# Second token group of a two-layer hybrid decoder: the trunk after the linear attention on two-part weights and data, and a layer norm written in place

## The chip, the cores and the metric

One core of one Trainium2 chip runs the whole step. The metric is the device time of one execution in microseconds (us). Five engines work side by side, each through its own queue in order: TensorE (PE in the rows, its weight loads PEld), VectorE (DVE), ScalarE (ACT), GpSimd (POOL) and SyncE (SP), which issues most transfers.

## The reference, cut to what matters

Two layers run over 512 prompt tokens and 64 sample tokens of width 1024. Each layer is a trunk and a channel mixer:

```
proj = x @ w_in + b_in                      # split among the mixers and the gates
A: windowed attention   B: GLA linear attention   C: causal pooling
oB = rmsnorm(gla) * silu(gb)
merged = sum_i sigmoid(gate_i) * (branch_i @ w_branch_i)
x = LN(alpha * x + merged @ w_out)
x = LN(alpha * x + peer(x))                 # product-key experts, top 16 of 16384
```

All of it is float32 in the reference.

## The kernel before

The tokens are cut into two groups. Group 0 is 256 prompt tokens and the 64 sample tokens (W = 320), group 1 the other 256 prompt tokens (W = 256, `G.fin`). In each layer `_p1` runs the trunk for group 0, the query of the channel mixer is computed for it, then `_p1` runs for group 1 and its query follows; then comes a long stretch over 128 blocks of experts.

A trunk weight is a tile of 128 x 1024 (512 KB, eight blocks of 128 x 128), fetched by `w_get` from the table `wall`, through a ring of three buffers per name. There are two ways to multiply with it (`passes`, L174; `mm_into`, L178):

- Group 0 uses two-part operands. `stream` (L132) loads `raw`, ScalarE casts it to `whi` (fp32r, L130), and VectorE forms `wlo = raw - whi` (L127). Data are split likewise into a high and a low part. Each of the eight blocks takes three matmuls: high by high, high by low, low by high. That is 24 matmuls per tile.
- Group 1 uses plain float32 (`G.nat`): `raw` goes to TensorE as it lands, with one float32 matmul per block. The trace shows each of these as two records.

The query tiles (`pq`) are split for both groups, on GpSimd in group 1.

The order of group 1's trunk: attention with its gate `ga` and its branch product `wa`; `_phase_gla` (qb, kb, vb and the chunked scan); `_phase_gla_out` (eight `gb` tiles, L573); `_branch` with eight `gbr` and eight `wb` tiles (L230); `_phase_pool` (eight `uc` tiles, L629, and two `wp` tiles used in parts, L615); `_branch` with eight `gc` and eight `wc` tiles; `_phase_out` (eight `wo` tiles, L742, then `_ln` and the transposes at L708). From `gb` on this is 58 tiles a layer.

While group 1's trunk runs, group 0's selection and spread run in the background: each `w_get` calls `tick`, which issues about one background step (`set_bg`, L1122, about 100 steps for about 100 tiles). A spread step is one comparison over 128 x 512 on VectorE (`jo`, L930), four of 128 x 128 (`io`, L936), four float32 matmuls (L940), and four ScalarE copies into `gst` (L942); every eighth step writes four `gst` tiles to memory (`gd`, L948), and each of these tiles has one buffer. Some steps also gather a row of experts (`uvr`) and weigh it on VectorE (L994, L1001). Background work stands behind the trunk in the planner's priorities, weight loads and splits stand ahead of it (`PRIO`, 95). The framework's planner sets the final order of every engine's queue before the run by its own estimates.

Of the kernel before, what the change touches and what calls it, by code (L numbers as in the profile page):

```python
# [10 lines left out]
F32 = mybir.dt.float32  # L11
F32R = mybir.dt.float32r
# [59 lines left out]
WPOS = {n: i for i, n in enumerate(PLAN)}  # L72
# [34 lines left out]
class Net:  # L107
# [59 lines left out]
    def w_get(self, l, name, pool=None):  # L167
        self.tick()
        with self.tc.high_priority(PRIO):
            return self.stream(self.I["wall"][l, WPOS[name]], self.nc.vector if self.G.smp else self.nc.gpsimd, pool,  # L170
                               whole=self.G.nat and name[0] != "pq")

    @staticmethod
    def passes(w):  # L174
# [45 lines left out]
def _gate(n, l, gname, m, th):  # L220
    psg = n.mm(n.w_get(l, (gname, m)), n.xs, n.G.W)
    b = BPOS[gname, m]
    n.nc.scalar.activation(th, psg, AF.Tanh, scale=0.5, bias=n.hb[:, b:b + 1])


def _branch(n, l, gname, wname, o, first):
    nc, W = n.nc, n.G.W
    with n.tc.tile_pool(name="br_" + gname, bufs=3, side="right" if gname == "gbr" else "left") as up:
        n.up = up
        for m in range(8):  # L230
            dst = n.merged[m // 4][:, m % 4, :]
            if not first:
                th = n.unit("th")
                _gate(n, l, gname, m, th)
            psb = n.mm(n.w_get(l, (wname, m)), o, W)
            if first:
                nc.vector.scalar_tensor_tensor(dst, dst, 1.0, psb, op0=OP.add, op1=OP.mult)
            else:
                nc.vector.scalar_tensor_tensor(th, th, 1.0, psb, op0=OP.add, op1=OP.mult)
                nc.gpsimd.tensor_tensor(dst, dst, th, op=OP.add)  # L240
# [440 lines left out]
def _ln(n, p, z, m, gb, out):  # L681
    nc = n.nc
    st = p.tile([128, 2, nc.vector.BN_STATS_DIM], F32, name="bst", bufs=2)
    for i in range(2):
        nc.vector.bn_stats(st[0:m, i, :], z[0:m, i * 512:(i + 1) * 512])
    mv = p.tile([128, 4], F32, name="mv", bufs=2)
    nc.vector.bn_aggr(mv[0:m, 0:2], st[0:m])
    nc.vector.tensor_scalar(mv[0:m, 2:3], mv[0:m, 1:2], LN_EPS, None, op0=OP.add)
    nc.scalar.activation(mv[0:m, 2:3], mv[0:m, 2:3], AF.Sqrt)
    nc.vector.scalar_tensor_tensor(z[0:m], z[0:m], mv[0:m, 0:1], gb[0:m, 0, :], op0=OP.subtract, op1=OP.mult)  # L690
    nc.vector.reciprocal(mv[0:m, 3:4], mv[0:m, 2:3])
    nc.vector.scalar_tensor_tensor(out[0:m], z[0:m], mv[0:m, 3:4], gb[0:m, 1, :], op0=OP.mult, op1=OP.add)
# [10 lines left out]
def _transpose_tok(n, x, m, new_ps, dsts):  # L703
    nc, c = n.nc, n.c
    for q in range(2):
        pt = new_ps()
        for k in range(4):
            nc.tensor.transpose(pt[:, k, 0:m], x[0:m, (4 * q + k) * 128:(4 * q + k + 1) * 128], c["ident"][0:m, 0:m])  # L708
        for xh, xl, c0 in dsts:
            if xl is None:  # L710
                nc.scalar.copy(xh[q][:, :, c0:c0 + m], pt[:, :, 0:m])
            else:
                n.split(xh[q][:, :, c0:c0 + m], xl[q][:, :, c0:c0 + m], pt[:, :, 0:m])


def _phase_out(n, l, xres, dsts):
    tc, nc, G = n.tc, n.nc, n.G
    mp = n.parts("m")
    for m in range(8):
        q, k = m // 4, m % 4  # L720
        nc.scalar.activation(mp[0][q][:, k, :], n.merged[q][:, k, :], AF.Copy, scale=0.5)
        if len(mp) > 1:
            nc.vector.scalar_tensor_tensor(mp[1][q][:, k, :], n.merged[q][:, k, :], 0.5, mp[0][q][:, k, :].bitcast(F32),
                                           op0=OP.mult, op1=OP.subtract)
    ms = [n.ks(t) for t in mp]
    if n.G.smp:
        nc.scalar.dma_start(n.O["s_pool"][l, :, 7:15, :], n.us.rearrange("(b s) c -> b s c", b=NB))
    with tc.tile_pool(name="out", bufs=1) as p:
        gb = _ln_rows(n, p, l, 1)
        zs = []  # L730
        for t, c0, m in G.tok:
            z = p.tile([128, 1024], F32, name=f"z{t}")
            nc.sync.dma_start(z[0:m], xres[t * 128:t * 128 + m, :])
            zs.append(z)
        def block(q, blk, tok):
            (t, c0, m), z = tok
            ps = n.pmm.tile([128, 512], F32, tag="mm", name="ps_wo", bufs=3)
            pa = n.passes(blk[0])
            for a, (wi, xi) in enumerate(pa):
                for k in range(8):  # L740
                    w = blk[k // 4][wi].rearrange("p (k c) -> p k c", k=4)[:, k % 4, :]
                    nc.tensor.matmul(ps[0:m, 0:256], ms[xi][k][:, c0:c0 + m], w,  # L742
                                     start=(a == 0 and k == 0), stop=(a == len(pa) - 1 and k == 7))
            zc = z[0:m, q * 256:(q + 1) * 256]
            nc.vector.scalar_tensor_tensor(zc, zc, ALPHA, ps[0:m, 0:256], op0=OP.mult, op1=OP.add)

        toks = list(zip(G.tok, zs))
        with ExitStack() as wctx:
            late = wctx.enter_context(tc.tile_pool(name="wlate", bufs=4)) if G.smp else None
            for qs in ((0,), (1,), (2, 3)) if G.smp else ((0,), (1,), (2,), (3,)):  # L750
                blks = [[n.w_get(l, ("wo", 2 * q + i), late if len(qs) > 1 else None) for i in range(2)] for q in qs]
                for tok in toks:
                    for q, blk in zip(qs, blks):
                        block(q, blk, tok)
        for (t, c0, m), z in zip(G.tok, zs):
            x = p.tile([128, 1024], F32, name="x1", bufs=2)
            _ln(n, p, z, m, gb, x)
            nc.scalar.dma_start(n.x1d[t * 128:t * 128 + m, :], x[0:m])
            _transpose_tok(n, x, m, lambda: n.sm("pt"), dsts(t, c0))


def _p1(n, l, G, xs, xres, dsts, opened=None):
    tc = n.tc
    n.G, n.xs = G, xs
    with tc.tile_pool(name="mg", bufs=1) as mp:
        n.merged = [mp.tile([128, 4, G.W], F32, name=f"merged{q}") for q in range(2)]
        with tc.tile_pool(name="oqa", bufs=2 if G.nat else 4) as n.op:
            o = _phase_attn(n, l)
            if G.smp:
                for i, nm in enumerate(("s_win_k", "s_win_v")):  # L770
                    n.nc.scalar.dma_start(n.O[nm][l].rearrange("b t h d -> b t (h d)")[:, 120:128, :],
                                          n.kvs[i].rearrange("(b s) c -> b s c", b=NB))
            _branch(n, l, "ga", "wa", o, True)
        with tc.tile_pool(name="oT", side="right", bufs=1) as op_:
            oT = [op_.tile([128, G.W], F32, name=f"oT{i}") for i in range(8)]
            _phase_gla(n, l, oT)
            with tc.tile_pool(name="oqb", side="right", bufs=2 if G.nat else 4) as n.op:
                o = _phase_gla_out(n, l, oT)
                _branch(n, l, "gbr", "wb", o, False)
        with tc.tile_pool(name="oqc", bufs=2 if G.nat else 4) as n.op:  # L780
            o = _phase_pool(n, l)
            _branch(n, l, "gc", "wc", o, False)
        if opened:
            opened()
        with tc.tile_pool(name="oqm", bufs=2 if G.nat else 4) as n.op:
            _phase_out(n, l, xres, dsts)
# [235 lines left out]
def tile_hybrid_step(ctx, tc, I, O, L):  # L1022
    nc = tc.nc
    n = Net(ctx, tc, I, O, L)
# [37 lines left out]
        return rc, lc, xa, x32  # L1062

    rc, xac, xa, x32 = open_layer(0)
    def load_x(p, g, xs):
        for k in range(8):
            src = I["xT"][:, k, g.c0:g.c0 + g.W]
            if g.nat:
                nc.sync.dma_start(xs[k // 4][:, k % 4, :], src)
            else:  # L1070
                r = p.tile([128, G0.W], F32, name="xr")
                nc.sync.dma_start(r[:, 0:g.W], src)
                n.split(xs[0][k // 4][:, k % 4, :], xs[1][k // 4][:, k % 4, :], r[:, 0:g.W])
            yield

    xc, xp = scope("xin", side="right", bufs=8)
    for _ in load_x(xp, G0, xa):
        pass
    n.set_bg([load_x(xp, G1, x32)], 0.2)

    for l in range(L):
# [48 lines left out]
        gb = _ln_rows(n, fp, l, 2)  # L1130
# [83 lines left out]
        ec.close()  # L1214
        if not last:
            rc, xac, xa, x32 = open_layer(l + 1)

        def put(z, t, m):
            if last:
# [10 lines left out]
        for t in range(3):  # L1230
            z = zp.tile([128, 1024], F32, name="zA", bufs=3)
            nc.sync.dma_start(z, n.x1d[t * 128:(t + 1) * 128, :])
            zs.append(z)
        for t in (3, 0, 1, 2):
            if t == 3:
                z = gat.z[0]
                nc.vector.scalar_tensor_tensor(z, gat.x[0], ALPHA, z, op0=OP.mult, op1=OP.add)
            else:
                z = zs[t]
# [161 lines left out]
```

## Time and profile before

| | us |
|---|---|
| median of three timed runs | 4894.38 (4884.02 to 4894.83) |
| the profiled execution, its own time | 4896.88 |
| its span, first to last instruction | 4895.1 |

The numbers of the profile are those of the one profiled execution. Its busy times are unions of an engine's records. TensorE's records overlap each other, so what a run of matmuls costs is read from start to start.

### The profile page before, as it was taken

What the parts mean: (1) busy time and instruction counts of PE and PEld (TensorE: products, weight loads), DVE (VectorE), ACT (ScalarE), POOL (GpSimd) and SP (SyncE); (2) the same over time, 40 slices, a digit from 0 to 9 for tenths busy, and PEclk for the clock granted to TensorE, in tenths of its full rate; (3) what the DMA queues carried; (4) which work ended last, traced back from release to release, by engine and by line L of the source; (5) the groups of instructions that cost most, each with busy time, mean ns of one, the idle gap of its engine ahead of it and who ended that gap; (6) DMA issues with size and microseconds to landing.
All of it is one profiled execution on the core that took longest, in us unless ns stands there. A gap on an engine that the chain in (4) does not pass through costs nothing. (4 is left out here: it accounts for less than half of the span.)

```text
span 4895.1 us, 68783 instructions
## 1 busy us (share of the span) xinstructions
PE 4619.8 (94%) x25204; PEld 4101.0 (84%) x25204; DVE 3698.0 (76%) x7119; ACT 1741.6 (36%) x3722; POOL 1555.6 (32%) x996
## 2 busy tenths in 40 slices
PE   7999999998879999999999999999988899999998
PEld 6879977787878999999878889777878789999997
DVE  5446598644789999999864455977448899999998
ACT  3424323322333333333343243233223333333333
POOL 0011001111555555555300110011115555555552
PEclk9979999999999999999999799999999999999999
DMA  4324525565559899999723345255554598999886
GB/s 147 113 97 144 176 92 211 180 218 183 169 210 342 322 326 332 329 324 330 272 90 114 101 143 168 88 216 207 201 199 161 221 332 324 331 324 332 323 326 233
DMA packets 363743, 1095.65 MB, mean 224 GB/s; under 512 B 28623, under 2 KB 168399, under 8 KB 313933
## 3 DMA queue, kind: packets, MB, share of 16 engines
q1 hardware_dynamic: 276336, 610.98, 36.8%
q0 software_dynamic: 55296, 402.68, 22.0%
q10 hardware_dynamic: 31772, 77.60, 4.3%
q8 instruction: 199, 3.26, 0.3%
q14 instruction: 140, 1.14, 0.1%
HBM read 1014.01 MB, written 77.52 MB: 223 GB/s over the span
## 5 line engine op out<-in xcount | busy, mean ns | idle before, releaser
L127 POOL TENSOR_TENSOR wlo<-raw,whi 128x1024 fp32r<-128x1024 f32 x288 | 853.1, 2963 | 855.9 <-ACT whi L130 800.4
L1152 PE MATMUL ps_h<-x1A,whi 128*128 128x384 f32 x4096 | 778.2, 342 | 31.2 <-ACT h L1155 28.3
L130 ACT CAST whi<-raw 128x1024 fp32r<-128x1024 f32 x522 | 545.1, 1048 | 673.9 <-PE ps_mm L182 328.5
L1152 PEld LDWEIGHTS ps_h<-x1A,whi 128*128 128x128 f32 x4096 | 731.1, 192 | 51.6 <-ACT h L1155 31.4
L1001 DVE SCALAR_TENSOR_TENSOR zB<-uvr,hc,zB 128x1024 f32<-128x1024 f32 x380 | 571.9, 1505 | 5.0
L994 DVE SCALAR_TENSOR_TENSOR uvr<-uvr,x1B 128x1024 f32<-128x1024 f32 x384 | 486.4, 1267 | 93.5 <-DMA uvr<-uv,gidx 93.1
L983 POOL DMA_INDIRECT uvr<-uv,gidx x384 | 429.6, 1119 | 394.9 <-DVE zB L1001 195.3
L127 DVE TENSOR_TENSOR wlo<-raw,whi 128x1024 fp32r<-128x1024 f32 x234 | 288.3, 1237 | 276.4 <-PE ps_mm L182 142.0
L1208 PE MATMUL y<-vh,wh 128*128 128x512 f32 x1536 | 477.4, 392 | 5.1 <-ACT vh L130 5.1
L1208 PE MATMUL y<-vl,wh 128*128 128x512 f32 x1536 | 477.4, 392 | 2.0 <-DVE vl L127 2.0
L1208 PE MATMUL y<-vh,wl 128*128 128x512 f32 x1536 | 475.1, 390 | 0.0
L182 PE MATMUL ps_mm<-xw,raw 128*128 128x256 f32 x1888 | 460.3, 385 | 7.0 <-ACT xg L579 3.5
L182 PE MATMUL ps_mm<-xa,whi 128*128 128x320 f32 x2400 | 422.8, 326 | 14.6 <-ACT xa L130 14.6
L1197 DVE TENSOR_TENSOR h<-h,gt 128x384 f32<-128x384 f32 x256 | 402.2, 1577 | 27.2 <-DMA gt<-gd 13.5
L182 PEld LDWEIGHTS ps_mm<-xa,whi 128*128 128x128 f32 x2400 | 377.9, 197 | 39.4 <-issue 19.1
L1152 PE MATMUL ps_h<-x1A,wlo 128*128 128x384 f32 x2048 | 400.4, 338 | 0.0
L182 PEld LDWEIGHTS ps_mm<-xw,raw 128*128 128x128 f32 x1888 | 345.0, 193 | 62.0 <-issue 15.9
L1152 PEld LDWEIGHTS ps_h<-x1A,wlo 128*128 128x128 f32 x2048 | 361.4, 189 | 0.2
L1208 PEld LDWEIGHTS y<-vl,wh 128*128 128x128 f32 x1536 | 288.7, 188 | 67.4 <-DVE vl L127 3.6
L1208 PEld LDWEIGHTS y<-vh,wl 128*128 128x128 f32 x1536 | 289.1, 188 | 63.1
L1208 PEld LDWEIGHTS y<-vh,wh 128*128 128x128 f32 x1536 | 286.4, 188 | 49.8 <-ACT vh L130 5.7
L130 ACT CAST wh<-h 128x384 fp32r<-128x384 f32 x256 | 130.7, 512 | 554.0 <-PE y L1208 534.0
(342 smaller groups left out, 7178.0 us busy)
## 6 DMA issues: line engine op xcount, KB each, us to landing
raw<-wall SPq DMA_DIRECT2D x468, 512.0 KB
raw<-ut SPq DMA_DIRECT2D x256, 512.0 KB
vr<-vt SPq DMA_DIRECT2D x256, 512.0 KB
gd<-gst ACTq DMA_DIRECT2D x96, 512.0 KB
gt<-gd SPq DMA_DIRECT2D x62, 768.0 KB
S<-state_gla SPq DMA_DIRECT2D x8, 1024.0 KB
s_gla<-S ACTq DMA_DIRECT2D x8, 1024.0 KB
uvr<-uv,gidx POOLq DMA_INDIRECT x384
```

The lines of the kernel that those rows point to most:

```text
L127: return eng.tensor_tensor(lo, src, hi.bitcast(F32), op=OP.subtract)
L130: return self.nc.scalar.copy(hi, src), self.sub_lo(lo, src, hi, eng)
L182: self.nc.tensor.matmul(ps[:, 0:W], w[wi][:, k * 128:(k + 1) * 128], xs[xi][k], start=(a == 0 and k == 0), stop=(a == len(pa) - 1 and k == ...
L983: self.n.nc.gpsimd.indirect_dma_start(out=r, out_offset=None, in_=self.n.I["uv"], in_offset=bass.IndirectOffsetOnAxis(ap=self.idx[t][:, s: ...
L994: nc.vector.scalar_tensor_tensor(r[:, 0:1024], r[:, 0:1024], 1.0, self.x[t], op0=OP.mult, op1=OP.mult, accum_out=hc[:, 0:1])
L1001: nc.vector.scalar_tensor_tensor(acc, r[:, 1024:2048], hc[:, 1:2], acc, op0=OP.mult, op1=OP.add)
L1152: nc.tensor.matmul(ps[:, 0:TD], wt[:, k * 128:(k + 1) * 128], x1k[xi][k], start=(a == 0 and k == 0), stop=(a == 2 and k == 7))
L1197: nc.vector.tensor_tensor(h3, h3, gt[:, :, i % 4, :], op=OP.mult)
L1208: nc.tensor.matmul(y[t][d], wt[:, ts], vt[:, d * 512:(d + 1) * 512], start=(j == 0 and a == 0), stop=(j == NE - 1 and a == 2))
```

## The change

For group 1, from the output of the linear attention on, `G.nat` is switched off: the weights `gb`, `gbr`, `wb`, `uc`, `wp`, `gc`, `wc` and `wo` are split into two parts, cast on ScalarE and subtracted on VectorE, and so are the data that meet them. The group's input `x32` is split into four new tiles `x2` (two high, two low, 4 KB a partition each) just after `_phase_gla`; they are released after the pooling branch. Through the existing branches on `G.nat`, the gated output `ob`, the pooling difference `d`, the projected `oc` and the merged `m` get a low part as well, and their rings hold four tiles instead of two. `pq` of group 1 stays on GpSimd; every other split is on VectorE. `_phase_out` of both groups writes the layer norm into `z` and no longer uses the tile `x1` (two buffers of 4 KB a partition).

```diff
@@ w_get
-            return self.stream(self.I["wall"][l, WPOS[name]], self.nc.vector if self.G.smp else self.nc.gpsimd, pool,
-                               whole=self.G.nat and name[0] != "pq")
+            return self.stream(self.I["wall"][l, WPOS[name]], self.nc.gpsimd if self.G.fin and name[0] == "pq" else self.nc.vector,
+                               pool, whole=self.G.nat and name[0] != "pq")
@@ _phase_out
-            x = p.tile([128, 1024], F32, name="x1", bufs=2)
-            _ln(n, p, z, m, gb, x)
-            nc.scalar.dma_start(n.x1d[t * 128:t * 128 + m, :], x[0:m])
-            _transpose_tok(n, x, m, lambda: n.sm("pt"), dsts(t, c0))
+            _ln(n, p, z, m, gb, z)
+            nc.scalar.dma_start(n.x1d[t * 128:t * 128 + m, :], z[0:m])
+            _transpose_tok(n, z, m, lambda: n.sm("pt"), dsts(t, c0))
@@ _p1
+    G.nat = G.fin
-    with tc.tile_pool(name="mg", bufs=1) as mp:
+    with tc.tile_pool(name="mg", bufs=1) as mp, ExitStack() as xc:
...
             _phase_gla(n, l, oT)
+            if G.fin:
+                xp = xc.enter_context(tc.tile_pool(name="x2", bufs=1))
+                x2 = [[xp.tile([128, 4, G.W], F32R, name=f"x2{i}{q}") for q in range(2)] for i in range(2)]
+                for q in range(2):
+                    n.split(x2[0][q], x2[1][q], n.x32[q])
+                G.nat, n.xs = False, [n.ks(t) for t in x2]
             with tc.tile_pool(name="oqb", side="right", bufs=2 if G.nat else 4) as n.op:
...
             _branch(n, l, "gc", "wc", o, False)
+        xc.close()
         if opened:
             opened()
@@ tile_hybrid_step, after each open_layer
+    n.x32 = x32
```

## Rows read from the trace of the kernel before

**Rows 1.** The profile's page, busy time of each engine over the whole span.
```profile
PE 4619.8 (94%) x25204; PEld 4101.0 (84%) x25204; DVE 3698.0 (76%) x7119; ACT 1741.6 (36%) x3722; POOL 1555.6 (32%) x996
```
**Rows 2.** Stretches of group 1's trunk, layer 0, then two of layer 1.
```profile
core 0: us, PE busy (x) PEld busy (x) DVE busy (x) ACT busy (x) POOL busy (x), PEclk, DMA share, GB/s
956.00:992.00 36.00, 32.48 (x144) 28.01 (x144) 30.08 (x56) 12.12 (x33) 4.27 (x6) 0.95 0.82 306
992.00:1049.00 57.00, 54.52 (x275) 48.08 (x274) 18.20 (x39) 8.03 (x34) 11.75 (x12) 1.00 0.71 259
1049.00:1100.00 51.00, 49.17 (x271) 43.29 (x270) 31.02 (x89) 16.19 (x61) 2.44 (x8) 1.00 0.47 158
1100.00:1167.00 67.00, 67.00 (x365) 60.43 (x364) 24.28 (x69) 15.51 (x67) 5.68 (x8) 1.00 0.47 159
1167.00:1213.00 46.00, 38.58 (x196) 33.73 (x195) 20.62 (x53) 9.87 (x40) 2.48 (x2) 0.89 0.52 178
...
3392.00:3428.00 36.00, 32.52 (x151) 27.98 (x150) 29.58 (x56) 12.37 (x34) 4.32 (x5) 1.00 0.84 307
...
3603.00:3649.00 46.00, 37.82 (x197) 33.17 (x196) 21.93 (x54) 9.83 (x39) 2.50 (x2) 0.93 0.53 177
```
**Rows 3.** Timeline of TensorE, group 1, float32 tiles back to back: start, length.
```profile
1042.18 3.62 PE L182 MATMUL ps_mm<-ob,raw 128*128 128x256 f32 x16
1045.63 3.62 PE L182 MATMUL ps_mm<-xw,raw 128*128 128x256 f32 x16
```
**Rows 4.** Timeline of TensorE, group 1's query, two-part tiles of the same width.
```profile
1257.56 2.17 PE L182 MATMUL ps_yr<-xb,whi 128*128 128x256 f32 x16
1259.56 1.12 PE L182 MATMUL ps_yr<-xb,wlo 128*128 128x256 f32 x8
1260.52 0.61 PE L805 MATMUL ps_sc<-key,qT 128*128 128x128 f32 x4
```
**Rows 5.** Groups on VectorE, group 0's trunk, 340 to 620 us: busy, mean ns.
```profile
L127 DVE TENSOR_TENSOR wlo<-raw,whi 128x1024 fp32r<-128x1024 f32 x63 | 77.9, 1238 | 83.4 <-PE ps_mm L182 50.6 <-ACT whi L130 32.7
L127 DVE TENSOR_TENSOR d<-d,d 128x320 fp32r<-128x320 f32 x8 | 4.0, 505 | 0.4 <-ACT d L130 0.4
```
**Rows 6.** Groups on ScalarE, the same stretch.
```profile
L130 ACT CAST whi<-raw 128x1024 fp32r<-128x1024 f32 x64 | 66.7, 1050 | 121.0 <-PE ps_mm L182 94.8 <-PE ps_wo L742 12.4 <-issue 10.3
L130 ACT CAST d<-d 128x320 fp32r<-128x320 f32 x8 | 3.6, 455 | 0.9 <-DVE d L657 0.9
```
**Rows 7.** Groups on VectorE, group 1's trunk, 960 to 1227 us.
```profile
L936 DVE TENSOR_SCALAR io<-ct,selT 128x128 f32<-128x128 f32 x148 | 45.0, 358 | 0.0
L930 DVE TENSOR_TENSOR jo<-ct,selT 128x512 f32<-128x512 f32 x37 | 25.8, 697 | 44.6 <-PE ps_hr L940 43.2 <-ACT selT L917 1.3
```
**Rows 8.** Waits of TensorE, 956 to 1213 us: total, times, longest.
```profile
PE ps_hr L940 <- ACT gst L942: 7.4, 1, 7.4
PE ps_mm L182 <- ACT xg L579: 3.5, 1, 3.5
PE ps_mm L182 <- DMA raw<-wall: 2.3, 1, 2.3
```
**Rows 9.** Waits of ScalarE, 956 to 1213 us.
```profile
ACT gst L942 <- DMA gd<-gst: 29.7, 10, 8.5
```
**Rows 10.** Waits of TensorE in group 0's trunk, 340 to 620 us, the longest two.
```profile
PE pt L667 <- POOL usc L666: 5.8, 8, 1.2
PE pt L708 <- DVE x L692: 2.9, 1, 2.9
```
**Rows 11.** Stretches with a loaded VectorE: group 1's attention, the experts, group 0's trunk.
```profile
600.00:900.00 300.00, 285.94 (x1456) 228.97 (x1456) 247.89 (x965) 96.43 (x255) 27.15 (x32) 0.98 0.45 154
1600.00:2000.00 400.00, 400.00 (x2033) 364.59 (x2031) 375.58 (x420) 156.23 (x263) 224.44 (x115) 1.00 0.90 326
340.00:620.00 280.00, 266.27 (x1744) 256.17 (x1745) 164.63 (x328) 110.67 (x171) 31.33 (x42) 0.94 0.44 148
```
**Rows 12.** The query's weight loads on TensorE: count, ns min/median/max.
```profile
L182 PEld LDWEIGHTS ps_yr<-xb,whi x512: 187/192/333, 1227.4 to 3722.5; 128*128 128x128 f32 x171
```

More of the change, by code (lines that the diff above doesn't have):

```diff
@@ L1216, in tile_hybrid_step @@
             rc, xac, xa, x32 = open_layer(l + 1)
+            n.x32 = x32
         def put(z, t, m):
```

## Prediction

> **What bounds the kernel now.** I read the page first: TensorE is busy for 94% of the span, VectorE for 76% and ScalarE for 36% [rows 1]. That is an average over unlike stages, so I cut the changed stage, from the first `gb` tile to the last `wo` product, into five stretches. The reader is to see there that TensorE fills most of each at nearly full granted clock while VectorE is well filled only in two of them, the `gb` and the `uc` stretch [rows 2]. The stage is 257 us long (956 to 1213 us), and layer 1 repeats it 2436 us later with nearly the same shares (its first and last of five stretches are shown). Then I looked at what TensorE waits for in it: one wait of 7.4 us for ScalarE's spread copies, one of 3.5 us for a gate, one of 2.3 us for a weight [rows 8]. So TensorE's own work sets the length, and about 13 us of waits come on top. The DMA engines are not the bound, at 0.47 to 0.82 of their time.
>
> **The change, part by part.**
>
> *TensorE, the gain.* Two float32 tiles of 16 records start 3.45 us apart (1042.18 and 1045.63) [rows 3]. A two-part tile of the same 256 columns takes 1260.52 - 1257.56 = 2.96 us for 24 records [rows 4]: more matmuls, each much shorter. So each tile saves 3.45 - 2.96 = 0.49 us. The 58 tiles of a layer (eight each of `gb`, `gbr`, `wb`, `uc`, `gc`, `wc`, `wo`, two `wp`) save 58 x 0.49 = 28.4 us, the two layers 56.8 us.
>
> The Trainium skill speaks against this in "TensorE: Matmul & The Clock Gate", under "The mechanism" of Part 3: it says that a weight load overlaps running matmuls only if it goes to other rows of the array. By that rule the eight extra weight loads of a tile would cost their full length. A load's record lasts 192 ns, yet 24 pairs of load and matmul took 2.96 us, 123 ns a pair [rows 4, 12]. The row contradicts the rule, since a pair takes less time than its load; by the rule a tile would lose about 1 us, by the row it gains 0.49.
>
> *VectorE, the cost.* Each tile adds one `wlo` of 1.238 us [rows 5]: 58 x 1.238 = 71.8 us a layer. The low parts of `ob`, `d`, `oc` and `m` are 32 operations; the same ones at 320 columns took 505 ns [rows 5], and at 256 columns I take 0.45, so 14.4 us. The two low parts of `x2` are as large as a `wlo`: 2.5 us. Sum 88.7 us a layer, in a stage where VectorE has 124.2 us now (30.08 + 18.20 + 31.02 + 24.28 + 20.62) [rows 2]. It will have 213 us of work in a stage that TensorE alone would finish in 257 - 28 = 229 us.
>
> *ScalarE.* 58 casts of 1.050 us are 60.9 us, two for `x2` 2.1 us, and 16 casts of `ob` and `d` at up to 0.455 us 7.3 us [rows 6]; `oc` and `m` are evicted there already. With today's 61.7 us [rows 2] that is 132 of 229 us. It has room, but its queue is in order and stands still for 29.7 us in ten waits for `gd` [rows 9], and casts will now stand behind those waits. Three `whi` buffers let two finished tiles lie ahead of TensorE, 2 x 2.96 = 5.9 us; only the longest wait, 8.5 us, is longer. TensorE already loses 7.4 us there now. I cost this at nothing; if the ring were empty at every wait, it could cost up to 29.7 - 7.4 = 22 us a layer.
>
> *Transfers.* Count and size stay. A `raw` buffer comes free when `wlo` is done instead of when TensorE is done, so loads can start earlier; the 2.3 us wait [rows 8] may vanish. Taken at nothing.
>
> *Layer norm in place, and the tile sizes.* The same instructions with another output address; it frees 8 KB a partition, which the two extra tiles of `m` use. The transposes still wait for the norm's last step, so nothing.
>
> *How much VectorE gives back.* I take each stretch with the new work in it. For `gb` with `gbr`/`wb` (93 us): VectorE 48.3 + 24 x 1.238 + 8 x 0.45 + 2.5 = 84.1 us; TensorE 93 - 24 x 0.49 = 81.2 us. For `uc`/`wp` (51 us): VectorE 31.0 + 10 x 1.238 + 16 x 0.45 = 50.6 us; TensorE 51 - 4.9 = 46.1 us. For `gc`/`wc` (67 us): VectorE 44.1, TensorE 59.2 us. For `wo` (46 us): VectorE 34.1, TensorE 42.1 us. So VectorE becomes the longer one in the first two, by 3 and 4.5 us even if it never pauses. It does pause. Among the experts, its best stretch with TensorE full, it is busy for 375.58 of 400 us, 94%; in group 1's attention, with the same background selection, for 247.89 of 300, 83%, while TensorE is at 95% [rows 11].
>
> At 94% the first two stretches take 84.1 / 0.94 = 89.5 and 50.6 / 0.94 = 53.8 us, and with 59.2 and 42.1 the stage takes 244.6 us, 12.4 us less than now. At 83% they take 101.3 and 61.0 us, and the stage is 263.6 us, 6.6 us longer. If VectorE hid everything, by background steps moving into the `gc` stretch where it has 15 us to spare, the stage would be 28.4 us shorter. I take 14 us a layer: about the 94% case, since weight splits stand ahead of the background in priority and some of the background can move, and it is also half of the full gain. Group 0's trunk, which uses the same ring of three and splits on VectorE, loses only 13.7 of 280 us on TensorE, and its longest waits are for other things [rows 10, 11]; but its VectorE is at 59% [rows 11], so it is no proof for 93%.
>
> *Sum.* 4896.88 - 2 x 14 = 4869 us for the profiled execution; it lies 2.5 us above the median of the runs, so **4866 us** against 4894.38.
>
> **The rivals.** A measurement of this kernel tells a change from none at about 0.3%, 14.7 us, so between 4879.7 and 4909.1 us nothing has changed.
>
> 1. *VectorE hides all of it.* TensorE is the bound throughout, the background shifts. For it: 213 us of work fit 229 us. Against it: two stretches where VectorE has more work than TensorE, and comparisons for the spread that already wait 43.2 us for TensorE's matmuls [rows 7], so the two queues are tied to each other step by step. Gain 2 x 28.4: 4838 us.
> 2. *The gain is eaten.* VectorE reaches about 87%, or ScalarE's waits for `gd` hit an empty ring. With x the busy share in the first two stretches, 134.7 / x + 101.3 = 257 gives x = 0.865 for no change. Near 4890 us.
> 3. *Slower: VectorE's queue becomes the bound in the `gb` and `uc` stretches.* A `wlo` stands behind a background comparison that waits for TensorE's spread matmul, which stands behind the tile that wants the `wlo`'s neighbour. For it: the 83% with the same kind of background in the attention stretch. Against it: TensorE was the fuller engine there, so 83% is not VectorE's limit. It decides from a share below 0.83 on: 134.7 / 0.83 + 101.3 is 6.6 us over the stage, 13 us for both layers; at 0.80 it is 12.7 us, 25 us for both, 4920 us.
> 4. *Weight loads don't overlap the matmuls.* If eight more loads of 192 ns [rows 12] cost their length, a tile loses 8 x 0.192 - 0.49 = 1.05 us, two layers 121 us: 5016 us. The query's two-part tiles exclude it, since 24 loads alone would take 4.6 us and the tile took 2.96 [rows 4]. This is the rule of the Trainium skill named above.
>
> **How the numbers follow.** Chances: the forecast, a gain of 15 to 45 us, 0.47; rival 1, over 45 us, 0.15; rival 2, 0.23; rival 3, 0.14; rival 4, 0.01. So faster 0.62, same 0.23, slower 0.15. The range runs from rival 1, 4838 us, to the upper end of no change, 4908 us; it leaves out rivals 3 and 4 and a sliver at the fast end. The likeliest case's own range is 4849 to 4880 us.
>
> **What the profile after would show.** The two-part tiles of `gb` to `wo` should start 2.96 us apart where nothing waits; if they are nearer to 3.45, the gain term is wrong. VectorE should be about 90% busy from `gb` to the last `uc` with 116 more `wlo` in all, and GpSimd should have no more than before. TensorE's waits should name `wlo` or `d` in the `uc` stretch, and few should name `whi`. If waits for `whi` behind `gst` copies dominate, rival 2 holds through ScalarE. If the spread's last matmuls come well after the last `wo` product, the background was pushed out of the stage, and its cost would appear before the query. A clock that falls in the `gb` stretch below today's 0.95 [rows 2] would add a loss that the sum leaves out, since TensorE's short pauses are not priced for it.

## The result and the profile after

The changed kernel takes 4847.77 us (median of five, 4839.26 to 4858.47) against 4894.83 us for the kernel before on the same chip (five runs, 4884.02 to 4917.03). The ratio is 0.9897, 95% interval 0.9872 to 0.9923: 47 us faster by the medians, 50 us by the ratio. A second measurement on another chip gave 0.9875 (0.9858 to 0.9892). Single executions were far slower than the rest (one of the second measurement's four took 6370 us); medians and ratios here are those of the others. The forecast was 4866 us, the range 4838 to 4908 us, so the time lies inside the range. The profiled execution of the changed kernel took 4858.47 us with a span of 4856.7 us.

The profile's page, busy time of each engine, to be read beside [rows 1]:

```profile
PE 4582.4 (94%) x26132; PEld 4105.7 (85%) x26132; DVE 3853.8 (79%) x7303; ACT 1869.3 (38%) x3874; POOL 1583.2 (33%) x996
```

TensorE has more instructions and less busy time. VectorE gained 156 us of work in all, and GpSimd has as many instructions as before. PEclk in the next rows is TensorE's mean granted clock: 1.00 is the upper level, 2.4 GHz, and a lower mean holds time at the lower one, 1.2 GHz.

The five stretches of group 1's trunk in layer 0 (`gb`, `gbr`/`wb`, `uc`/`wp`, `gc`/`wc`, `wo`), as in [rows 2]; below them the linear attention's scan before `gb`, and the whole stage from the first `gb` product to the last `wo` product:

```profile
core 0: us, PE busy (x) PEld busy (x) DVE busy (x) ACT busy (x) POOL busy (x), PEclk, DMA share, GB/s
968.00:995.00 27.00, 27.00 (x224) 26.86 (x223) 24.52 (x39) 20.62 (x44) 0.30 (x1) 0.99 0.79 278
995.00:1052.00 57.00, 51.12 (x419) 49.73 (x418) 52.23 (x85) 25.31 (x56) 17.93 (x14) 1.00 0.82 296
1052.00:1100.00 48.00, 41.97 (x322) 39.87 (x321) 44.95 (x110) 27.71 (x83) 3.04 (x9) 0.95 0.52 173
1100.00:1163.00 63.00, 62.43 (x509) 62.12 (x508) 53.23 (x109) 30.86 (x80) 10.60 (x7) 0.96 0.58 193
1163.00:1197.00 34.00, 30.78 (x245) 30.37 (x244) 24.59 (x52) 17.73 (x49) 5.08 (x3) 0.95 0.68 247
898.10:968.82 70.72, 60.66 (x338) 49.78 (x337) 52.70 (x112) 34.43 (x97) 18.80 (x19) 0.90 0.46 152
968.82:1196.02 227.20, 212.47 (x1707) 208.27 (x1706) 197.76 (x390) 121.27 (x310) 35.67 (x33) 0.97 0.67 232
```

VectorE is busy for 121.7 of the first 132 us (92%) and for 87% of the stage. The `gb` stretch shrank from 36 to 27 us and `wo` from 46 to 34 us. No product of a changed tile runs in the scan, but the first splits do: VectorE has 7.2 us more work there than before, and the scan is longer.

TensorE's timeline in the `gb` stretch, start and length, to be read beside [rows 3, 4]:

```profile
971.52 2.08 PE L182 MATMUL ps_mm<-x,whi 128*128 128x256 f32 x16
973.44 1.12 PE L182 MATMUL ps_mm<-x,wlo 128*128 128x256 f32 x8
974.40 1.84 PE L182 MATMUL ps_mm<-x,whi 128*128 128x256 f32 x14
```

Two-part tiles start 2.88 us apart. Waits of TensorE in the stage, the largest totals (total, times, longest), to be read beside [rows 8]. Lines 936 to 942 of the kernel before are 943 to 949 here.

```profile
PE ps_hr L947 <- DVE io L943: 3.2, 3, 2.3
PE pt L662 <- ACT u_ext L640: 2.9, 2, 1.7
PE ps_hr L947 <- ACT gst L949: 2.8, 2, 2.2
PE ps_mm L182 <- DVE th L239: 2.6, 1, 2.6
PE ps_mm L182 <- ACT ob L130: 1.9, 1, 1.9
```

No wait for `wlo`, `whi` or `d` is among them. VectorE's spread comparison `jo`, whose idle time before it was 44.6 us [rows 7], now has

```profile
L937 DVE TENSOR_TENSOR jo<-ct,selT 128x512 f32<-128x512 f32 x37 | 27.8, 753 | 4.1 <-PE ps_hr L947 3.7
```

ScalarE's waits in the same stretch:

```profile
ACT whi L130 <- DMA raw<-wall: 20.2, 11, 3.5
...
ACT gst L949 <- DMA gd<-gst: 6.5, 7, 2.4
```

The casts now wait for weights as they land, 11 times, and the waits for `gd` fell from 29.7 us [rows 9] to 6.5.

The table cuts group 1's part of each layer at its own events in the profiled executions. "Again" is the second measurement of the same kernel.

| us, layer 0 / layer 1 | before | after | again |
|---|---|---|---|
| attention and vb | 225.0 / 223.2 | 223.2 / 230.0 | 229.0 / 222.7 |
| scan, to the first `gb` product | 65.3 / 59.7 | 70.7 / 74.9 | 76.4 / 65.0 |
| `gb` to the last `wo` product | 255.4 / 253.8 | 227.2 / 231.1 | 227.0 / 230.5 |
| last `wo` product to the query | 15.8 / 17.2 | 12.6 / 12.4 | 12.6 / 12.6 |
| query, to the experts | 64.4 / 63.1 | 57.7 / 56.7 | 57.2 / 55.8 |
| sum of both layers | 1242.8 | 1196.5 | 1188.8 |

The stage gained 51 to 52 us in both layers together, the stretch behind it 21 to 22 us, and the scan gave back 16 to 21 us. The rest of the span has none of the changed tiles. It varies by some 20 us between the profiled executions of this document (3641 to 3660 us), so small differences are read from the timed runs and not from one profile.

### The profile page after: what moved, and what is told of

It is laid out like the page before. It is cut to its first block, busy times and chain, and to the rows that moved or that the text cites. A ratio compares the mean times of both kernels' runs of the same rounds, so it can differ in the third digit from the quotient of the medians.

```text
span 4856.7 us, 71125 instructions
## 1 busy us (share of the span) xinstructions
PE 4582.4 (94%) x26132; PEld 4105.7 (85%) x26132; DVE 3853.8 (79%) x7303; ACT 1869.3 (38%) x3874; POOL 1583.2 (33%) x996
## 5 line engine op out<-in xcount | busy, mean ns | idle before, releaser
L130 ACT CAST whi<-raw 128x1024 fp32r<-128x1024 f32 x638 | 666.4, 1048 | 727.8 <-PE ps_mm L182 363.1
L127 DVE TENSOR_TENSOR wlo<-raw,whi 128x1024 fp32r<-128x1024 f32 x350 | 432.2, 1240 | 293.2 <-PE ps_mm L182 144.5
L1003 ACT ACTIVATE hc<-hc 128x1 f32<-128x1 f32 x384 | 77.5, 203 | 639.8 <-DVE uvr L1001 625.6
L127 DVE TENSOR_TENSOR vl<-vr,vh 128x1024 fp32r<-128x1024 f32 x256 | 316.0, 1235 | 0.0
```

The costliest lines, as they stand in the source:

```text
L127: return eng.tensor_tensor(lo, src, hi.bitcast(F32), op=OP.subtract)
L130: return self.nc.scalar.copy(hi, src), self.sub_lo(lo, src, hi, eng)
L1003: nc.scalar.activation(hc[:, 1:2], hc[:, 0:1], AF.Gelu)
```

## The experiments

Each was timed in rounds against the kernel before on its own chip; that kernel's median was 4900 to 4902 us there.

**The layer norm alone** (float32 trunk as before).

```diff
-            x = p.tile([128, 1024], F32, name="x1", bufs=2)
-            _ln(n, p, z, m, gb, x)
+            _ln(n, p, z, m, gb, z)
```

> Only the layer norm in place, in the kernel before; the trunk of group 1 stays float32. My theory: the norm's instructions and waits are the same, so no change, a ratio of 0.997 to 1.003, and 0 us of the 38 to 47 us gained. Rival: the shorter stretch from the last wo product to the query (15.9 to 12.8 us in layer 0, 17.3 to 12.5 in layer 1) comes from the norm in place; then this run has that shorter stretch and gains about 8 us.

Measured: 4905.83 us, ratio 1.001 (0.9995 to 1.0026). The query part stayed at 63.4 us in both layers. The norm in place does nothing to the time, and what follows can be measured on top of it.

**Two-part from the pooling on**, without `gb`, `gbr` and `wb`: 34 tiles a layer in place of 58. The block that makes `x2` moves behind the branch.

```diff
                 o = _phase_gla_out(n, l, oT)
                 _branch(n, l, "gbr", "wb", o, False)
+        if G.fin:
+            ...
+            G.nat, n.xs = False, [n.ks(t) for t in x2]
```

> The change, but from the pooling branch on: gb, gbr and wb stay float32 (24 of 58 tiles a layer), x2 is split after the second branch. If the scan stretch of group 1 (first vb product to first gb product, 117.4 and 112.0 us before, 122.8 and 127.8 after) became longer because the splits of x2 and of the first gb tiles stand in its queues, it is back at 112 to 118 us here, and the lost gain of 24 x 0.53 x 2 = 25 us comes back in good part: 4848 to 4858 us. If it became longer by the granted clock alone, this run stays about 25 us behind the whole change: 4865 to 4875 us.

Measured: 4852.88 us, 0.991 (0.9885 to 0.9934). 34 tiles bring nearly all that 58 bring. The stage took 237.3 and 238.0 us, 7 to 10 us more than with all tiles, but the scan 66.7 and 59.7 us, as before. So in these profiles `gb`, `gbr` and `wb` earn in the stage about what the scan gives back; what makes the scan longer is taken up further down.

**Two-part for `wo` and `m` alone**, eight tiles a layer.

```diff
+        if G.fin:
+            G.nat = False
         if opened:
             opened()
```

> Only the eight wo tiles of group 1 (and m) in two parts, everything before them float32, norm in place. TensorE saves 8 x 0.57 = 4.6 us a layer. If the 10 us a layer between the last wo product and the first expert product come from the wo tiles freeing their raw buffers after the subtraction, they come here too: 25 to 30 us faster than before, and that stretch at 69 to 72 us. If they need the whole trunk to be faster, so that the background is done earlier, the stretch stays at 77 to 80 us and the gain at 8 to 12 us.

Measured: 4870.38 us, 0.9935 (0.9922 to 0.9947). Eight tiles bring 32 us, where TensorE's saving of 0.57 us a tile makes 9 us for both layers. The stretch behind the last `wo` product fell by 20.4 us in both layers together, nearly all that it falls by in the whole change. Both possible reasons are at work here, though: the `wo` tiles free `raw` early, and the spread ends 10 us ahead of the last `wo` product, as in the whole change. TensorE's waits in that stretch, layer 0, in the kernel before and in this one:

```profile
PE pt L708 <- DVE x L692: 5.8, 1, 5.8
PE ps_sc L805 <- DMA key<-keysT: 5.0, 2, 3.4
PE pt L708 <- DVE mv L687: 2.9, 1, 2.9
```

```profile
PE pt L708 <- DVE z L692: 7.0, 1, 7.0
PE ps_h L1156 <- DVE s L797: 1.4, 1, 1.4
PE ps_yr L182 <- DVE xb L127: 1.4, 1, 1.4
PE ps_sc L808 <- DMA key<-keysT: 0.8, 1, 0.8
```

The wait for the query's keys goes from 5.0 to 0.8 us, and the two waits for the norm (8.7 us) become one (7.0 us).

**The weights' low part left out of the work.** The 58 tiles use `whi` in place of `wlo`, so VectorE has 72 us less to do a layer; TensorE's matmuls are as many as in the change.

```diff
+        if eng is None:
+            self.nc.scalar.copy(hi, raw)
+            return hi, hi
         self.split(hi, lo, raw, eng)
```

> The whole change, but VectorE makes no low part of the 58 weight tiles of group 1 (the high part is used in its place, so the weights' low part is left out of the result); TensorE does the same matmuls, VectorE has 72 us less a layer. My forecast's cost term (VectorE gives back 14 us a layer): 25 to 30 us faster than the whole change, about 4820 us. Rival 1 (VectorE hides it): within 12 us of the whole change, 4836 to 4855 us.

Measured: 4841.97 us, 0.9889 (0.9863 to 0.9914), against 0.9897 and 0.9875 for the whole change. The stage with VectorE relieved:

```profile
956.00:1188.52 232.52, 210.32 (x1708) 206.47 (x1707) 136.88 (x340) 121.84 (x313) 31.62 (x35) 0.96 0.65 232
```

VectorE is at 59% and the stage is no shorter than with 87%. From scan to last `wo` product it takes 292.7 and 299.0 us, the whole change 297.9 and 306.0, again 303.4 and 295.5. That is 5 us a layer less on average, no more than one kernel's two profiles differ by, and part of it can be that `raw` is freed sooner here. The timed ratios show no gain from relieving VectorE.

**Each `wlo` formed twice.** `nc_hi` is the same cast on ScalarE.

```diff
+        if eng is None:
+            eng = self.nc.vector
+            self.sub_lo(lo, raw, self.nc_hi(hi, raw), eng)
+            self.sub_lo(lo, raw, hi, eng)
+            return hi, lo
```

> The whole change, but VectorE forms each low part of group 1's 58 weight tiles twice, so 66 to 72 us more work a layer. From the first gb product to the last wo product VectorE has 200 us of work in 229 us now, and would have 268. If VectorE is the bound once its work exceeds TensorE's, the stretch becomes 268 to 290 us and the time rises by 80 to 120 us for both layers, to 4925 to 4965 us. If background work can still move out of the stretch, it rises by less than 60 us.

Measured: 4948.3 us, 1.0099 (1.0083 to 1.0115), about 100 us above the whole change. The stage, and TensorE's longest waits and those for `wlo` in it:

```profile
969.69:1248.88 279.19, 236.94 (x1716) 225.49 (x1714) 263.54 (x454) 121.67 (x310) 50.20 (x33) 0.90 0.54 184
```

```profile
PE ps_hr L956 <- DVE io L952: 12.8, 16, 2.7
PE ps_mm L191 <- ACT th L232: 7.2, 6, 4.5
PE pt L671 <- ACT u_ext L649: 6.9, 5, 2.2
PE ps_mm L191 <- DVE wlo L127: 3.2, 5, 1.8
```

Here VectorE is the bound: 263.5 of 279.2 us, 94%, and TensorE waits for it at many places. This is the ceiling that the prediction took from the experts' stretch. The change itself stays below it.

**The weight splits of group 1 on GpSimd** in place of VectorE.

```diff
-... self.nc.gpsimd if self.G.fin and name[0] == "pq" else self.nc.vector, ...
+... self.nc.gpsimd if self.G.fin else self.nc.vector, ...
```

> The whole change with all weight splits of group 1's trunk on GpSimd instead of VectorE; the splits of the data stay on VectorE. A subtraction takes 2.95 us there, a two-part tile on TensorE 2.88, so GpSimd would need 58 x 2.95 + 41 = 212 us of a 229 us stretch and TensorE would wait for wlo: 10 to 40 us slower than the whole change. Rival: VectorE's load is what costs, then relief of VectorE makes it equal or up to 10 us faster.

Measured: 4932.83 us, 1.0056 (1.0043 to 1.0069), nearly 90 us above the whole change and far past the 10 to 40 us expected. The stage takes 276.8 us. VectorE lost 58 subtractions a layer and still shows more busy time than in the changed kernel:

```profile
972.61:1249.43 276.82, 226.59 (x1707) 221.04 (x1707) 225.90 (x339) 121.20 (x312) 169.82 (x90) 0.90 0.56 193
```

Its groups by line show why; first the spread's comparison in the changed kernel, then in this one:

```profile
L943 DVE TENSOR_SCALAR io<-ct,selT 128x128 f32<-128x128 f32 x148 | 43.1, 346 | 0.0
```

```profile
L943 DVE TENSOR_SCALAR io<-ct,selT 128x128 f32<-128x128 f32 x152 | 94.6, 677 | 0.0
...
L1008 DVE SCALAR_TENSOR_TENSOR zB<-uvr,hc,zB 128x1024 f32<-128x1024 f32 x8 | 19.1, 2389 | 0.1
```

The same instruction takes 677 ns in place of 346 while GpSimd is busy for 61% of the stage. The granted clock of 0.90 is not the reason: with `wlo` formed twice, at the same 0.90 and with GpSimd busy for 18%, it took 373 ns. It was expected that TensorE would wait for `wlo`; instead it waits for what VectorE now makes late. Its largest wait in the stage:

```profile
PE ps_hr L947 <- DVE io L943: 15.2, 5, 8.3
```

**A fourth `raw` buffer on float32**, with the norm in place that frees the memory for it.

```diff
-raw = pool.tile([128, 1024], F32, tag="raw", name="raw")
+raw = pool.tile([128, 1024], F32, tag="raw", name="raw", bufs=4 if pool is self.wp else None)
```

> Float32 trunk as before, norm in place, and a ring of four raw weight buffers instead of three, so that loads run further ahead of TensorE. Theory of transfers: the query of group 1 became 6.5 us shorter per layer because raw buffers come free earlier, so with more of them TensorE's waits for the keys (5.0 us in layer 0) vanish here too, and the time falls by 10 to 15 us for both layers. Rival: the query became shorter because the background had been finished earlier; then this run keeps the 5 us of waits for the keys and gains under 4 us.

Measured: 4883.20 us, 0.9964 (0.9948 to 0.998), 16 us. The query part fell to 58.9 and 60.6 us, and the wait for keys to 1.6 us in layer 0. A deeper ring alone gives 8 us of the 13 that the two-part `wo` tiles gave in the query, but 6 of these are lost before it (19.8 and 19.5 us from the last `wo` product to the query). The profiled execution, 4896.99 us, was the slowest of the eleven, so it does not show where the 16 us come from.

**A faster background on float32**, with the norm in place: with `NW = 88.0` the background is done earlier.

```diff
-NW = 100.0
+NW = 88.0
```

> Float32 trunk, norm in place, and background steps issued 100/88 times as fast, so that the spread ends before the last wo product. Theory: in the changed kernel the stretch from the last wo product to the first expert product is 9 to 10 us shorter per layer (70 instead of 80) because the background was finished earlier; then it falls to 70 to 73 us here too and the time by 12 to 19 us. Rival: it is shorter because the two-part wo tiles free their raw buffers at once, so that the query's weights and keys load earlier; then it stays at 78 to 80 us and the time within 8 us.

Measured: 4904.51 us, 1.0009 (0.9998 to 1.002). The spread's last matmul lies 38 us ahead of the last `wo` product (1.8 us behind it in the kernel before), and the way from there to the query falls to 11.8 and 12.1 us, as in the changed kernel. The query stays at 61.6 and 63.3 us. What is won there is lost in the attention (178.9 and 178.1 us against 172.8 and 170.7) and the scan.

**The whole change with a fourth `raw` buffer**, paid for by one `ext` buffer of group 1.

```diff
+raw = pool.tile([128, 1024], F32, tag="raw", name="raw", bufs=4 if pool is self.wp else None)
...
-u = p.tile([128, EXT], F32, tag="ext", name="u_ext", bufs=5)
+u = p.tile([128, EXT], F32, tag="ext", name="u_ext", bufs=4 if G.fin else 5)
```

> The whole change with four raw buffers instead of three (and four instead of five buffers for the pooling sums of group 1, to make room). The float32 trunk gained 17.6 us from the fourth. If what it gained there is the same thing that the change gains by freeing raw buffers after the subtraction, a fourth adds little here: within 8 us of the whole change. If the two are separate, it is 12 to 18 us faster than the whole change, about 4832 us.

Measured: 4815.34 us, 0.9819 (0.9806 to 0.9831), 29 us below the whole change on the same chip (4844.30 us). That is more than either expectation, and the fastest version here. Its scan and its stage in layer 0:

```profile
960.30:1184.52 224.22, 208.38 (x1715) 203.79 (x1713) 203.01 (x400) 121.74 (x312) 41.95 (x36) 1.00 0.67 238
897.74:960.30 62.56, 55.75 (x332) 46.42 (x331) 47.05 (x102) 32.49 (x94) 14.07 (x17) 0.95 0.46 160
```

From scan to last `wo` product it takes 286.8 and 291.5 us, 28 us a layer less than before. ScalarE's waits for `raw` in that stretch, 20.2 us in layer 0 of the changed kernel, are down to this:

```profile
ACT whi L130 <- DMA raw<-wall: 3.6, 3, 2.4
```

**The whole change again**, as the common reference of the second chip.

> The whole change once more, for a second profile beside the other kernels of this call. From the first scan product of group 1 to its first gb product it took 70.7 and 74.9 us, against 65.3 and 59.7 before and 66.7 and 59.7 with the change from the pooling branch on. If the splits of x2 and of the first gb tiles in VectorE's queue do this, it is again over 68 us in both layers. If a low granted clock did it (0.82 in layer 1), layer 1 comes back to 60 to 66 us.

Measured: 4844.30 us, 0.9875 (0.9858 to 0.9892). Its scan shows how far that part varies at the same program; the two layers:

```profile
905.14:981.55 76.41, 67.54 (x338) 55.62 (x337) 51.75 (x112) 34.43 (x97) 18.49 (x19) 0.80 0.41 138
3316.07:3381.04 64.97, 56.14 (x338) 46.60 (x337) 51.06 (x110) 34.14 (x97) 17.38 (x18) 0.97 0.45 157
```

76.4 us at a granted clock of 0.80, 65.0 at 0.97, with the same work in both. So layer 1 came back, as expected if the clock is the cause, and layer 0 did not. For comparison layer 1 in the first profile of the change, then the scan without any split, both layers, in the kernel before and with two parts from the pooling on:

```profile
3314.67:3389.53 74.86, 66.59 (x338) 54.98 (x337) 51.77 (x112) 34.44 (x97) 18.50 (x19) 0.82 0.42 140
890.88:956.21 65.33, 59.18 (x337) 48.72 (x336) 45.49 (x106) 29.15 (x91) 14.04 (x17) 0.92 0.35 123
3332.80:3392.45 59.65, 54.70 (x337) 45.67 (x336) 45.57 (x106) 29.03 (x91) 14.04 (x17) 1.00 0.38 135
898.20:964.92 66.72, 60.57 (x337) 50.12 (x336) 45.45 (x106) 29.00 (x91) 14.01 (x17) 0.90 0.33 120
3311.73:3371.42 59.69, 54.70 (x337) 45.70 (x336) 45.55 (x106) 29.05 (x91) 14.02 (x17) 1.00 0.38 135
```

Without splits the scan too is 59.7 us long at a granted clock of 1.00 and 65 to 67 us at 0.90 and 0.92.

## Why the prediction was right, and where its sizes were off

The time lies inside the range, but the gain of 47 us is past the 15 to 45 us of the likeliest case and in the band given to rival 1, with a chance of 0.15. The forecast of 28 us came out too small by terms that the sum did not hold, and these partly cancel each other.

*TensorE.* The mechanism was right and the term a little small: 2.88 us a tile, so 0.57 us saved, 33 us a layer, against 28.4. The fourth rival is out. 24 pairs of load and matmul took 2.88 us, 120 ns a pair, less than one load's record [rows 12], so eight more loads did not add their length. The sentence of the Trainium skill's "TensorE: Matmul & The Clock Gate" (Part 3, "The mechanism"), that a load overlaps running matmuls only if it goes to other rows of the array, is not what this kernel shows. The same section also lets a load into the background weight buffer go ahead of running matmuls, which would agree; no run here shows which it is.

*VectorE.* The work was sized well: 197.8 us in the stage, and 7 us more in the scan before it, against a forecast of 213; busy for 92% from `gb` to the last `uc`, where about 90% was said. What failed is the step "How much VectorE gives back", which took 14 us a layer from the share at which VectorE would become the bound. Without its 58 subtractions the kernel is faster by no more than about 5 us a layer; with twice as many it costs some 50 us a layer. So 94% is the ceiling, as taken, but the stage does not meet it: by the code the splits stand ahead of the background in priority, and the background fills what is left. This is the first rival's mechanism, and its price, 4838 us, lies just below the fastest run, 4839.26 us. Of its counter-argument, the comparisons tied to TensorE's matmuls, 3.7 us of waits are left, where [rows 7] had 43.2.

*Where TensorE's 33 us a layer went.* From scan to last `wo` product the whole change gains 16.4 us a layer (mean of two layers in two profiled executions). That this is close to the forecast of 14 is luck, since VectorE, the forecast's reason, accounts for 5 us at most. With a fourth `raw` buffer 28 us arrive. On float32 that buffer leaves this part no shorter, so it matters here with the two-part tiles alone, which are used faster. What it changes is seen when the granted clock is set beside the length, here for layer 0 / layer 1. Length times granted clock is an estimate of the time that the stretch would take at the upper level throughout, if TensorE sets its pace.

| scan to last `wo` product | us | PEclk | us times PEclk |
|---|---|---|---|
| before | 320.7 / 313.5 | 0.96 / 0.98 | 308 / 307 |
| float32, fourth `raw` buffer | 320.1 / 318.1 | 0.96 / 0.96 | 307 / 305 |
| whole change | 297.9 / 306.0 | 0.95 / 0.92 | 283 / 281 |
| whole change again | 303.4 / 295.5 | 0.93 / 0.98 | 282 / 290 |
| without the subtractions | 292.7 / 299.0 | 0.97 / 0.95 | 284 / 284 |
| whole change, fourth `raw` buffer | 286.8 / 291.5 | 0.99 / 0.98 | 284 / 286 |

By that estimate the change gains some 24 us a layer, with three buffers or four, with or without the subtractions. So of the missing 17 us about 8 are time in which TensorE had the lower clock level, and the nearly 12 us that the fourth buffer brings in this stretch are of this kind; the other 9 arrive in none of these kernels. The timed runs agree on the clock: over the whole execution it was 0.957 to 0.963 in the eight runs of the change, 0.963 to 0.964 in the five with four buffers. The casts' waits for `raw` fell from 20.2 to 3.6 us at the same time. That these waits are what lowers the clock is not shown, and one run speaks against it: without the subtractions the casts wait for `raw` for 1.3 and 2.8 us in the stage, and its granted clock is 0.96 and 0.95 all the same.

*Transfers, "taken at nothing".* This is a mis-sized term, on both sides: casts wait for `raw` in the stage, and behind it the query is 13 to 15 us shorter in both layers together. The query's wait for keys has vanished, a deeper ring on float32 cuts the same part, and a faster background alone leaves it nearly as long. That `raw` is free after the subtraction and not after TensorE is argued from the code. Part of the gain is again the clock: 0.95 and 1.00 in the query, where it was 0.93 and 0.92. The 3 to 5 us a layer from the last `wo` product to the query fit a background that ended 10 us ahead of that product, since a faster background alone gave the same.

*The scan.* No step of the prediction priced it. Three `gb` splits and those of `x2` run there, and it is 5 to 15 us longer a layer. Most of that is the clock: length times granted clock is 60 us in each of the four scans without splits shown above (59.7 to 60.1), and 61 to 64 us in the four of the whole change. The splits thus cost some 2 us a layer at most; the rest is time at the lower level. What lowers the clock in the scan stays open, since the same program had 0.80 in one layer and 0.97 in the other.

*ScalarE.* Costed at nothing, rightly: no wait for `whi` stands among TensorE's, and the waits for `gd` shrank. The second rival, which put a price there, did not happen, nor did the third.

*What the profile after would show.* Tiles 2.96 us apart or less: yes. Waits that name `wlo` or `d` in the `uc` stretch: no; they name the spread's `io`, `u_ext` and `gst`. The spread's end: 10 us ahead of the last `wo` product. The clock in the `gb` stretch: 0.99, above 0.95; it fell instead to 0.95 and 0.96 in `uc` and `gc`, from 1.00.

Still open: some 9 us a layer of TensorE's gain that arrive in none of the kernels; what lowers the clock, and so by what way the fourth buffer acts; and whether `x2` could be split ahead of the scan, which was not tried.

## What to carry to other kernels

An engine that would be busy for about 90% of a stage is not yet its bound if what must be early has priority and the rest can slip; double the suspected work and remove it, and see at which end the time moves. When each tile is used faster, look at once at the depth of the ring that feeds it: here one more buffer brought 29 us on top of the change's 50, and 16 us on float32. Before a difference between two profiles is given a cause, set the granted clock beside the length; here it made up half of what seemed to be missing, and most of the scan's loss. Look also behind the changed stage, at the first loads of the next one: here that was worth 13 to 15 us.

## What the runs showed of the hardware unexpectedly

VectorE is slower beside GpSimd's subtractions. With GpSimd busy for 61% of the stage, a 128x128 comparison on VectorE took 677 ns in place of 346, and a 128x1024 multiply-add 2389 ns in place of 1333; with GpSimd busy for 18% at the same granted clock the comparison took 373 ns. Moving 72 us of work a layer to GpSimd left VectorE with 28 us more busy time than it had with that work.

A VectorE that is the bound and runs in order reached 94% here, in the doubled-split stage, as in the experts' stretch [rows 11].

The length of one and the same stretch follows the granted clock closely: the scan without splits took 59.7 us at 1.00, 65.3 us at 0.92 and 66.7 us at 0.90, and with the change's splits 65.0 us at 0.97 and 76.4 us at 0.80.
